# Hybrid S5 and mLSTM trunk: PSUM operands for VectorE, stored high and low parts, and block products on GpSimd

## The chip, the core and the metric

The kernel runs on one core of one Trainium2 chip. A core has TensorE (PE, matrix products), VectorE (DVE, elementwise work with one or two inputs), ScalarE (ACT, one input through a function), GpSimd (POOL, elementwise work) and SyncE (SP, which here only issues DMAs). Operands lie in SBUF or in PSUM. [...]

The metric is the device time of one execution in microseconds (us); lower is better. Every run here is the median of several executions where more than one was made.

## The reference

Two layers, each of one mixer, over 512 tokens of width 1024, all in fp32. Cut to what matters:

```python
h = rms_norm(x, norm_gain) * (1 + scale) + shift          # scale, shift, gate from silu(c) @ w_mod
ssm_in, ssm_gate, m_in, m_o, m_gate = split(h @ w_in)     # 1024 columns each
# S5: 64 groups of 16 channels, each with a complex diagonal state of 64
y = gelu(Re(C @ scan(a, B @ ssm_in)) + d * ssm_in)
y = y * sigmoid(y @ w_glu + b_glu)
ssm_y = rms_norm(y, out_gain) * silu(ssm_gate)
# mLSTM: 4 heads of 256
xc = silu(causal_conv4(m_in) + conv_b)
q, k, v = xc @ wq, xc @ wk / 16, m_in @ wv
i_pre, f_pre = [q|k|v] @ w_gates
num, den = stabilised matrix memory of (q, k, v, i_pre, log_sigmoid(f_pre))
hn = layer_norm(num / max(|den|, exp(-m)) * sigmoid(m_o)) * m_gain
m_y = (hn + skip * xc) * silu(m_gate)
x = x + gate * ([ssm_y | m_y] @ w_out)
```

A last `rms_norm` closes the trunk.

## The kernel before

**Tiling.** Activations are held with channels in the 128 lanes and the 512 tokens along the free axis, eight such tiles for a width of 1024. [...] `split` makes the two parts: ACT writes `hi`, then DVE or POOL subtracts. The low parts of all weights are POOL's. Of the activations, the kinds in the table `LOW` are POOL's, the others DVE's.

**S5.** The recurrence runs over chunks of 8 tokens: 64 chunks, 63 steps in order, each step four DVE operations on 128x64 elements (`scan`). Before it, the powers of `a` are multiplied into B for blocks of 8 groups (`u_prep`, three products and sums on 128x1024: B'), and into C (`u_outp`: C', which waits in DRAM until the output stage). PE forms the chunk inputs from B' (`v5`) and the outputs from C' (`y5`).

**mLSTM.** `min_u` projects, convolves by four taps and applies silu; `v_u` forms v; v and the convolved rows go to DRAM in fp32, and `qk`, `s_u` and `t_u` read them back later; `qk` and `s_u` split them again into high and low parts. `gate_rows` works on 4x512 rows. `pv` ends with a layer norm, whose inverse square root is a Newton iteration on DVE (`rsqrt_steps`).

**GLU.** `y_load`, `glu` and `s_gate` read the S5 output, which is stored by (step in the chunk, chunk), through a view that turns it into token order.

**Order of work.** The work is cut into units, named in the table `ORDER`, one string for each layer: IN and SI (S5 input), MI (mLSTM input), PR (B'), V (chunk inputs), VU and CU (v and convolved rows), CP and CV (C' on POOL and on DVE), GR and GC (gate rows and columns), SC (eight steps of the recurrence), O (output gate), GM and GS (gates of the two branches), QK, SU, PV, TU (the parts of a head), Y (S5 output), YL and GL (GLU), SN and SG (its norm and gate), OM, OS, OA and OB (output projection), MD and MC (adaLN columns), NH (input of the next layer). What a unit does ahead of its first `yield` is issue in an earlier unit's place (`@n`: n units earlier). PE, ACT, POOL and SP run their instructions in just this order; a scheduler sets the order of DVE's. Loads and most stores are issued by SP; a store is issued some units after its data was asked for (the `LAG_` constants), and SP waits there if the data is not ready, with all later loads behind it. Weights are fetched two ahead (`LA`). All PSUM tiles come from one pool of eight banks.

## Time and profile before

| What | Value |
| --- | --- |
| time, median of 3 runs | 1303.7 us (1298.79 to 1307.14) |
| the profiled execution | span 1301.3 us from the first to the last instruction; the page gives no other time of it, and the median lies 2.4 us above this span |
| mean granted TensorE clock | 0.916 |
| busy: PE, DVE, POOL, ACT | 1123.8, 988.9, 612.2, 511.4 us |
| recurrence, layer 0 and layer 1 (first to last step) | 249.6 to 365.0 us, 898.6 to 1000.1 us |
| B' on DVE, layer 0 and layer 1 | 101.9 to 215.8 us, 713.9 to 866.0 us |
| DMA | 213.34 MB, 164 GB/s on average |

The span can be cut by what the kernel does: start (0 to 95 us), input stage of layer 0 (95 to 250), recurrence (250 to 365), heads and S5 output (365 to 520), GLU (520 to 580), output projection (580 to 684), S5 input of layer 1 (684 to 762), its input stage (762 to 898), recurrence (898 to 1000), heads (1000 to 1147), GLU and output projection (1147 to 1301). A view by windows gives each engine's busy time in such stretches. An instruction that has started and is held back by the hardware counts as busy, so a long duration of a small instruction has to be compared with the shortest of its kind.

### The profile page before, as it was taken

Reading aid. Unit: us, or ns where it says so; the run is one execution under the profiler, and the core shown is the slowest. Engines: PE = TensorE matmul, PEld = TensorE weight load, DVE = VectorE, ACT = ScalarE, POOL = GpSimd, SP = SyncE. Lnnn points to the kernel's source line nnn. Section 1 sums busy time; section 2 is a strip of 40 time slices with the busy share of each in tenths; the row PEclk is TensorE's granted clock in tenths of the full one; section 3 lists DMA queues with packets and bytes.
Section 4 is the critical chain, followed back from the end, with each engine's and each line's share of the span. In section 5 each row is a group of like instructions: output and inputs, shape, how many; then the busy total and the mean of one; then the engine's idle time right before and its main releaser. Section 6 shows DMA issues by size and latency. Waiting matters only on the chain.

```text
span 1301.3 us, 17201 instructions
## 1 busy us (share of the span) xinstructions
PE 1123.8 (86%) x6020; PEld 966.2 (74%) x6020; DVE 988.9 (76%) x1892; ACT 511.4 (39%) x821; POOL 612.2 (47%) x333
## 2 busy tenths in 40 slices
...
GB/s 307 155 190 146 135 90 117 164 121 118 257 186 168 155 247 172 267 236 180 73 205 98 93 173 181 118 94 198 198 94 158 208 202 218 194 227 153 123 73 65
DMA packets 274338, 213.34 MB, mean 164 GB/s; under 512 B 63820, under 2 KB 239436, under 8 KB 274252
## 3 DMA queue, kind: packets, MB, share of 16 engines
...
## 4 chain that ended last, share of the span: by engine, by line
PE 36%; DVE 34%; issue 11%; POOL 6%; DMA 5%; SPq 4%; ACT 3%; DVEq 0%; POOLq 0%; ACTq 0%
DVE sc_a L925 4%; DVE st L928 4%; DVE macc L751 2%; DVE cv L799 2%; DMA wr_in<-in_w_in_dram 2%; DVE sc_b L926 2%; DVE sc_a L927 2%; PE ps_ga L411 2%; PE ps_ga L412 2%; PE ps_os L412 2%; PE ps_os L413 2%; PE ps_ga L413 2%; PE ps_os L411 2%; DVE bu L682 2%; PE ps_om L412 2%
## 5 line engine op out<-in xcount | busy, mean ns | idle before, releaser
L127 POOL TENSOR_TENSOR wl_in<-wr_in,wh_in 128x1024 fp32r<-128x1024 f32 x57 | 142.5, 2502 | 279.1 <-ACT wh_in L126 263.9
L126 ACT ACTIVATE wh_in<-wr_in 128x1024 fp32r<-128x1024 f32 x57 | 60.1, 1057 | 118.2 <-DMA wr_in<-in_w_in_dram 83.1
L411 PE MATMUL ps_ga<-hh,wh_in 128*128 128x512 f32 x256 | 104.4, 408 | 0.0
L412 PE MATMUL ps_ga<-hh,wl_in 128*128 128x512 f32 x256 | 102.9, 402 | 0.7 <-POOL wl_in L127 0.7
L413 PE MATMUL ps_ga<-hl,wh_in 128*128 128x512 f32 x256 | 102.4, 400 | 0.0
L411 PE MATMUL ps_o<-wh_o,hh 128*128 128x256 f32 x256 | 73.8, 288 | 14.3 <-ACT wh_o L126 14.3
L413 PE MATMUL ps_o<-wl_o,hh 128*128 128x256 f32 x256 | 74.0, 289 | 6.8 <-POOL wl_o L127 6.8
L412 PE MATMUL ps_o<-wh_o,hl 128*128 128x256 f32 x256 | 73.4, 287 | 0.0
L127 POOL TENSOR_TENSOR wl_o<-wr_o,wh_o 128x1024 fp32r<-128x1024 f32 x16 | 41.1, 2568 | 57.4 <-ACT wh_o L126 47.7
L127 POOL TENSOR_TENSOR vl<-vf,vh 128x1024 fp32r<-128x1024 f32 x8 | 17.6, 2202 | 94.6 <-ACT vh L126 59.9
L411 PEld LDWEIGHTS ps_o<-wh_o,hh 128*128 128x128 f32 x256 | 50.1, 196 | 15.2 <-ACT wh_o L126 14.9
L978 DVE SCALAR_TENSOR_TENSOR gath<-gath,ps_ga 128x512 f32<-128x512 f32 x32 | 21.8, 682 | 50.7 <-ACT gath L977 50.6
L925 DVE TENSOR_TENSOR sc_a<-a8r,st 128x64 f32<-128x64 f32 x126 | 56.8, 451 | 3.9
L412 PE MATMUL ps_gl<-yh,wl_gl 128*128 128x512 f32 x128 | 52.6, 411 | 6.6 <-POOL wl_gl L127 6.6
L412 PEld LDWEIGHTS ps_ga<-hh,wl_in 128*128 128x128 f32 x256 | 49.4, 193 | 11.7 <-POOL wl_in L127 1.1
L413 PEld LDWEIGHTS ps_ga<-hl,wh_in 128*128 128x128 f32 x256 | 49.2, 192 | 11.6
L411 PEld LDWEIGHTS ps_ga<-hh,wh_in 128*128 128x128 f32 x256 | 49.5, 193 | 11.1 <-issue 0.2
L928 DVE TENSOR_TENSOR st<-sc_a,sc_b 128x64 f32<-128x64 f32 x126 | 54.1, 429 | 3.6
L413 PEld LDWEIGHTS ps_o<-wl_o,hh 128*128 128x128 f32 x256 | 49.8, 195 | 7.7 <-POOL wl_o L127 7.7
L412 PE MATMUL ps_mi<-hh,wl_in 128*128 128x512 f32 x128 | 52.2, 408 | 3.7 <-POOL wl_in L127 3.7
L413 PE MATMUL ps_gl<-yl,wh_gl 128*128 128x512 f32 x128 | 52.8, 412 | 2.6 <-DVE yl L127 1.8
L700 PE MATMUL kps<-pair,bt 128*128 128x144 f32 x256 | 42.9, 332 | 13.1 <-DVE pair L691 13.0
...
## 6 DMA issues: line engine op xcount, KB each, us to landing
...
```

Source lines behind the costliest of these rows:

```text
L126: S.activation(out=hi, in_=src, func=AF.Copy)
L127: (eng or V).tensor_tensor(out=lo, in0=src, in1=r32(hi), op=ALU.subtract)
L411: PE.matmul(ps, lhsT=w[0], rhs=a[0], start=first, stop=False)
L412: PE.matmul(ps, lhsT=w[1], rhs=a[0], start=False, stop=False)
L413: PE.matmul(ps, lhsT=w[0], rhs=a[1], start=False, stop=last)
L682: V.tensor_tensor(out=bu, in0=pw_[:, 1, gs, :].unsqueeze(3).to_broadcast(shp), in1=bt_in[:, 1].unsqueeze(2).to_broadcast(shp), op=ALU.mult)
L700: PE.matmul(kps[:, 144 * e:144 * e + 144], lhsT=bt[:, 2 * i + e].rearrange("p k c -> p (k c)"), rhs=pair[:, i, 16 * e:16 * e + 144], start ...
L751: V.scalar_tensor_tensor(out=acc, in0=wt, scalar=silc[:, k:k + 1], in1=acc, op0=ALU.mult, op1=ALU.add)
L799: V.scalar_tensor_tensor(out=cv[:, sh:], in0=xm[:, j, 0:T - sh], scalar=vcol(l, "conv_w", tap * 8 + m), in1=cv[:, sh:], op0=ALU.mult, op1= ...
L925: V.tensor_tensor(out=ta, in0=a8r[:, l], in1=st[:, n - 1], op=ALU.mult)
L926: V.tensor_tensor(out=tb, in0=a8i[:, l], in1=st[:, n - 1, ::-1, :], op=ALU.mult)
L928: V.tensor_tensor(out=st[:, n], in0=ta, in1=tb, op=ALU.add)
```

## The change

1. **One input in PSUM.** Of most DVE operations with two inputs, one input is now a PSUM tile. `scan` copies its two coefficient tiles into a PSUM bank and writes both products there. The convolution reads the projection's PSUM tile, whose bank stays in use until the silu and the split are done. `gate_rows`, the Newton iteration, the attention weights, the GLU products, the head's output products and `next_h` are changed in the same way. [...]
2. **High and low parts in DRAM.** `min_u` and `v_u` split their results at once; v is stored as two tensors and the convolved rows as three (full, high, low). `qk` and `s_u` load the parts and split nothing.
3. **GLU by (step, chunk).** `y_load` and `glu` keep the stored order, and the S5 gate is written in it; the turn into token order is made in `s_gate`.
4. **B' and C' on POOL.** `u_prep` makes B' by five POOL instructions (one product of 128x1024, two of 128x512, two sums of 128x512). All C' blocks are POOL's (CV is gone), and in `ORDER` the C' blocks stand behind the input stage, among the steps of the recurrence.
5. **Moved to ACT.** One tap and the bias of the convolution, the last scaling of the layer norm, and a copy of two S5 inputs to PSUM; ACT's copy of the S5 output is gone.

```diff
 ORDER (layer 0)
-    IN7 F0@5 F2 F1@3 PR0 MI0 F3 MI1 PR1 UB MI2@4 V0 VU0 CP0 PR2 MI3 V1 PR3 MI4 V2@5 VU1 CU0 PR4 MI5@1
+    IN7 F0@5 F2 F1@3 PR0 MI0 F3 MI1 PR1 VU0 UB CU0 MI2@4 V0 PR2 MI3 V1 VU1 PR3 CU1 MI4 V2@5 PR4
...
-LOW = {"p2", "p3", "s0", "v", "wk", "wq", "wv", "xm", "y1"}
+LOW = {"wk", "wq", "wv", "y1"}
...
 def u_prep(l, b):
-        V.tensor_tensor(out=bt, in0=pw_[:, 0, gs, :].unsqueeze(3).to_broadcast(shp),
-                        in1=bt_in[:, 0].unsqueeze(2).to_broadcast(shp), op=ALU.mult)
-        V.tensor_tensor(out=bu, in0=pw_[:, 1, gs, :].unsqueeze(3).to_broadcast(shp),
-                        in1=bt_in[:, 1].unsqueeze(2).to_broadcast(shp), op=ALU.mult)
-        V.tensor_tensor(out=bt, in0=bt, in1=bu, op=ALU.add)
+        GP.tensor_tensor(out=bt, in0=pw_[:, 0, gs, :].unsqueeze(3).to_broadcast(shp),
+                         in1=bc_in[:, 0].unsqueeze(2).to_broadcast(shp), op=ALU.mult)
+        for i in range(2):
...
+            GP.tensor_tensor(out=bu, in0=pw_[:, 1, gh, :].unsqueeze(3).to_broadcast(shh),
+                             in1=bc_in[:, 1, hs_].unsqueeze(2).to_broadcast(shh), op=ALU.mult)
+            GP.tensor_tensor(out=bt[:, hs_], in0=bt[:, hs_], in1=bu, op=ALU.add)
...
 def min_u(m):
-            S.activation(out=xm[:, j], in_=ps, func=AF.Copy)
-            V.tensor_scalar(out=cv, in0=xm[:, j], scalar1=vcol(l, "conv_w", 3 * 8 + m),
-                            scalar2=vcol(l, "conv_b", m), op0=ALU.mult, op1=ALU.add)
+            S.activation(out=xmp[h][0][:, j], in_=ps, func=AF.Copy)
+            S.activation(out=cv, in_=ps, func=AF.Identity, scale=vcol(l, "conv_w", 3 * 8 + m),
+                         bias=vcol(l, "conv_b", m))
+            V.tensor_tensor(out=xmp[h][1][:, j], in0=ps, in1=r32(xmp[h][0][:, j]), op=ALU.subtract)
             for tap in range(3):
-                V.scalar_tensor_tensor(out=cv[:, sh:], in0=xm[:, j, 0:T - sh],
+                V.scalar_tensor_tensor(out=cv[:, sh:], in0=ps[:, 0:T - sh],
...
             yield
-            V.scalar_tensor_tensor(out=xc[h][:, j], in0=th, scalar=1.0, in1=cv, op0=ALU.add, op1=ALU.mult)
+            V.scalar_tensor_tensor(out=ps, in0=ps, scalar=1.0, in1=cv, op0=ALU.add, op1=ALU.mult)
+            yield
+            split(xcp[h][0][:, j], xcp[h][1][:, j], ps)
+            S.activation(out=xc, in_=ps, func=AF.Copy)
+            store(Xd[l][0][h][:, j], xc, LAG_X)
...
 def scan(n0, n1):
+                s5["sc"] = ptile([P, 4, 2, 32], "scp")
...
-                V.tensor_tensor(out=ta, in0=a8r[:, l], in1=st[:, n - 1], op=ALU.mult)
-                V.tensor_tensor(out=tb, in0=a8i[:, l], in1=st[:, n - 1, ::-1, :], op=ALU.mult)
-                V.tensor_tensor(out=ta, in0=ta, in1=st[:, n], op=ALU.add)
-                V.tensor_tensor(out=st[:, n], in0=ta, in1=tb, op=ALU.add)
+                V.tensor_tensor(out=ta, in0=ar, in1=st[:, n - 1], op=ALU.mult)
+                V.tensor_tensor(out=tb, in0=ai, in1=st[:, n - 1, ::-1, :], op=ALU.mult)
+                V.tensor_tensor(out=tv, in0=ta, in1=st[:, n], op=ALU.add)
+                V.tensor_tensor(out=st[:, n], in0=tb, in1=tv, op=ALU.add)
...
 def qk(h):
-            split(xch, xcl, xr, low("xr"))
+            ld(out=r32(xch), in_=Xd[l][1][h])
+            ld(out=r32(xcl), in_=Xd[l][2][h])
...
 def glu(m):
-            V.scalar_tensor_tensor(out=yv, in0=view(th), scalar=1.0, in1=yv, op0=ALU.add, op1=ALU.mult)
+            S.activation(out=ps, in_=ps, func=AF.Tanh, scale=0.25, bias=hb_glu[:, l, m:m + 1])
+            V.scalar_tensor_tensor(out=ps, in0=ps, scalar=1.0, in1=yv, op0=ALU.add, op1=ALU.mult)
...
-            V.scalar_tensor_tensor(out=yv, in0=view(gt), scalar=hgain[:, l, m:m + 1], in1=yv,
+            V.scalar_tensor_tensor(out=yv, in0=gt, scalar=hgain[:, l, m:m + 1], in1=ps,
```

**DVE at the first steps of the recurrence, layer 0.** Before, with the gate rows in between (`row_lf`, `row_m`, `row_i`, `row_b`, `brow`; `sc_a` and `sc_b` are the two products of a step, `st` the states):

```order
L1022 SCALAR_TENSOR_TENSOR row_lf<-row_f,row_la 4x512
L928 TENSOR_TENSOR st<-sc_a,sc_b 128x64
L1023 SCALAR_TENSOR_TENSOR row_m<-row_lf,row_i 4x512
L1024 SCALAR_TENSOR_TENSOR row_b<-row_lf,zeros 4x512
L1028 CAST brow<-zeros 36x512
L1025 TENSOR_TENSOR row_i<-row_i,row_b 4x512
L925 TENSOR_TENSOR sc_a<-a8r,st 128x64
L1026 TENSOR_TENSOR row_b<-row_b,row_m 4x512
L926 TENSOR_TENSOR sc_b<-a8i,st 128x64
```

The same place after, where `scp` is the PSUM tile of the recurrence and `gps` that of the gates:

```order
L1034 SCALAR_TENSOR_TENSOR gps<-gps,row_la 4x512
L1035 SCALAR_TENSOR_TENSOR row_m<-gps,row_i 4x512
L1036 SCALAR_TENSOR_TENSOR gps<-gps,zeros 4x512
L1040 CAST brow<-zeros 36x512
L1037 TENSOR_TENSOR row_i<-row_i,gps 4x512
L1038 TENSOR_TENSOR gps<-gps,row_m 4x512
L933 TENSOR_TENSOR sc_v<-scp,st 128x64
L1041 CAST brow<-gps 4x512
L934 TENSOR_TENSOR st<-scp,sc_v 128x64
```

The gate rows now come within the first step instead of within the eleventh, and each row with two inputs has `gps` or `scp` among them.

**POOL in the input stage of layer 0.** Before, around the low part of the second head's input (`xml`); `wl_in` is the low part of a projection weight, `wvl` that of a v weight, `cp` and `cu` are C':

```order
L127 TENSOR_TENSOR wl_in<-wr_in,wh_in 128x1024
L127 TENSOR_TENSOR xml<-xm,xmh 128x1024
L127 TENSOR_TENSOR wvl<-wv,wvh 128x512
L127 TENSOR_TENSOR wl_in<-wr_in,wh_in 128x1024 x2
L127 TENSOR_TENSOR xml<-xm,xmh 128x1024
```

After, from the second head's v weight on (`bt` and `bu` are B'):

```order
L127 TENSOR_TENSOR wvl<-wv,wvh 128x512
L127 TENSOR_TENSOR wl_in<-wr_in,wh_in 128x1024
L670 TENSOR_TENSOR bt<-pw,bc_in 128x1024
L678 TENSOR_TENSOR bu<-pw,bc_in 128x512
L680 TENSOR_TENSOR bt<-bt,bu 128x512
L678 TENSOR_TENSOR bu<-pw,bc_in 128x512
L680 TENSOR_TENSOR bt<-bt,bu 128x512
L127 TENSOR_TENSOR wl_in<-wr_in,wh_in 128x1024
```

A block of B' now stands between two weights' low parts, and the low part of the head's input has left the queue.

**POOL in the recurrence of layer 0.** Before, between the first four weights of the output gate (`wl_o`) there is one block of C':

```order
L735 TENSOR_TENSOR cp<-cp,cu 128x512
L127 TENSOR_TENSOR wl_o<-wr_o,wh_o 128x1024
L127 TENSOR_TENSOR wl_in<-wr_in,wh_in 128x1024
L127 TENSOR_TENSOR wl_o<-wr_o,wh_o 128x1024
L731 TENSOR_TENSOR cp<-tw,ct_in_2330 128x512
```

After, a second one stands between the third and the fourth:

```order
L734 TENSOR_TENSOR cp<-cp,cu 128x512
L127 TENSOR_TENSOR wl_o<-wr_o,wh_o 128x1024
L127 TENSOR_TENSOR wl_in<-wr_in,wh_in 128x1024
L730 TENSOR_TENSOR cp<-tw,ct_in_2113 128x512
L732 TENSOR_TENSOR cu<-tw,ct_in_2113 128x512
L734 TENSOR_TENSOR cp<-cp,cu 128x512
```

Over the whole recurrence of layer 0 the queue holds eight blocks of C' instead of four; in layer 1 five instead of one.

More of the change, by code (lines that the diff above doesn't have):

```diff
@@ L145, in rsqrt_steps @@
             yield
-    def rsqrt(out, x, shape):
-        for _ in rsqrt_steps(out, x, shape):
-            pass
     ident = const.tile([P, P], F32, name="ident")
@@ L786, in min_u @@
             if j == 0:
-                xms[h] = mt([P, 2, T], name="xm")
-                xc[h] = mt([P, 2, T], name="xc")
+                xmp[h] = mt([P, 2, T], F32R, name="xmh"), mt([P, 2, T], F32R, name="xml")
             w = weight(l, "in", 2 * KT + m)
@@ L859, in v_u @@
         def v_u(h):
-            xmh = mt([P, 2, T], F32R, name="xmh")
-            xml = mt([P, 2, T], F32R, name="xml")
-            split(xmh, xml, xms[h], low("xm"))
+            xmh, xml = xmp[h]
             wv = sw_([P, 2, DH], "wv")
@@ L878, in v_u @@
                             j == 0, j == 1)
-                S.activation(out=v[:, 2 * t2:2 * t2 + 2, :], in_=vps, func=AF.Copy)
-            sto(out=Vd[l][h], in_=v)
+                split(vh[:, 2 * t2:2 * t2 + 2, :], vl[:, 2 * t2:2 * t2 + 2, :], vps)
+            for i, t_ in enumerate((vh, vl)):
+                store(Vd[l][i][h], r32(t_), LAG_V)
             gate_mm(h, 0, xmh, xml)
         def c_u(h):
-            store(Xd[l][h], xc[h], LAG_X)
-            xch = mt([P, 2, T], F32R, name="xch")
-            xcl = mt([P, 2, T], F32R, name="xcl")
-            split(xch, xcl, xc[h], low("xc"))
             yield
-            gate_mm(h, 1, xch, xcl)
+            gate_mm(h, 1, *xcp[h])
+            for i, t_ in enumerate(xcp[h]):
+                store(Xd[l][1 + i][h], r32(t_), LAG_X)
         ub = []
@@ L921, in scan @@
             st = s5["st"]
[L922 to L928 removed]
+            if n0 == 1:
+                s5["sc"] = ptile([P, 4, 2, 32], "scp")
+                V.tensor_copy(out=s5["sc"][:, 0], in_=a8r[:, l])
+                V.tensor_copy(out=s5["sc"][:, 1], in_=a8i[:, l])
+            ar, ai, ta, tb = (s5["sc"][:, i] for i in range(4))
+            for n in range(n0, n1):
+                tv = small.tile([P, 2, 32], F32, tag="sc_v", name="sc_v")
+                V.tensor_tensor(out=ta, in0=ar, in1=st[:, n - 1], op=ALU.mult)
+                V.tensor_tensor(out=tb, in0=ai, in1=st[:, n - 1, ::-1, :], op=ALU.mult)
+                V.tensor_tensor(out=tv, in0=ta, in1=st[:, n], op=ALU.add)
+                V.tensor_tensor(out=st[:, n], in0=tb, in1=tv, op=ALU.add)
             yield
```

184 lines of the change are left out of this document (93 added, 91 removed).

## The prediction

> **What bounds the kernel now.** I read the page's busy times and chain first, then an order-of-time view of DVE and POOL in the recurrence, then the source view of single lines, then the stages by windows.
>
> ```profile
> span 1301.3 us, 17201 instructions
> PE 1123.8 (86%) x6020; PEld 966.2 (74%) x6020; DVE 988.9 (76%) x1892; ACT 511.4 (39%) x821; POOL 612.2 (47%) x333
> PE 36%; DVE 34%; issue 11%; POOL 6%; DMA 5%; SPq 4%; ACT 3%; DVEq 0%; POOLq 0%; ACTq 0%
> ```
>
> PE and DVE share the chain almost equally, so no one engine bounds the whole; the bound changes by stage. The next view shows what a DVE instruction costs in the recurrence (start, duration), quiet first, then beside POOL.
>
> ```profile
> 294.93 0.22 DVE L925 TENSOR_TENSOR sc_a<-a8r,st 128x64 f32<-128x64 f32 x1
> 295.07 0.22 DVE L926 TENSOR_TENSOR sc_b<-a8i,st 128x64 f32<-128x64 f32 x1
> 295.20 0.22 DVE L927 TENSOR_TENSOR sc_a<-sc_a,st 128x64 f32<-128x64 f32 x1
> 295.46 0.23 DVE L928 TENSOR_TENSOR st<-sc_a,sc_b 128x64 f32<-128x64 f32 x1
> 295.71 0.23 DVE L925 TENSOR_TENSOR sc_a<-a8r,st 128x64 f32<-128x64 f32 x1
> ...
> 299.12 2.38 POOL L127 TENSOR_TENSOR wl_in<-wr_in,wh_in 128x1024 fp32r<-128x1024 f32 x1 [8.62 <-ACT wh_in L126]
> 299.16 2.42 DVE L927 TENSOR_TENSOR sc_a<-sc_a,st 128x64 f32<-128x64 f32 x1
> ```
>
> A quiet step takes 0.78 us from start to start. The same instruction, started 0.04 us after a POOL subtraction of 2.38 us, lasts 2.42 us: it stood until POOL was done. Which instructions this strikes is seen from shortest, median and longest duration of a line (ns):
>
> ```profile
> L925 DVE TENSOR_TENSOR sc_a<-a8r,st x126: 206/225/2431, 89.0 to 999.4; 128x64 f32<-128x64 f32 x126
> L964 DVE SCALAR_TENSOR_TENSOR yt<-gq,yt x16: 679/690/1909, 397.7 to 1124.1; 128x512 f32<-128x512 f32 x16
> L978 DVE SCALAR_TENSOR_TENSOR gath<-gath,ps_ga x32: 669/684/691, 232.9 to 1146.3; 128x512 f32<-128x512 f32 x32
> L1274 DVE SCALAR_TENSOR_TENSOR nx<-ps_om,modc,xo x16: 726/740/752, 587.7 to 1248.1; 128x512 f32<-128x512 f32 x16
> ```
>
> The first two read SBUF twice and are held up to 2.4 us; the last two have one input in PSUM and, over 48 instances beside the same POOL, never are. That is what the change makes of most DVE work. What it can bring depends on what stands next in each stage (columns: length; busy PE, weight loads, DVE, ACT, POOL; clock; DMA share; GB/s):
>
> ```profile
> 95.00:250.00 155.00, 132.44 (x730) 117.80 (x731) 119.99 (x166) 59.06 (x102) 66.56 (x32) 0.87 0.56 121
> 250.00:365.00 115.00, 77.57 (x483) 69.24 (x481) 111.21 (x271) 27.07 (x36) 64.42 (x39) 0.83 0.50 165
> 365.00:520.00 155.00, 147.53 (x829) 128.96 (x830) 113.06 (x232) 85.32 (x153) 50.42 (x29) 0.93 0.69 192
> 520.00:580.00 60.00, 51.11 (x199) 39.17 (x198) 56.30 (x64) 24.47 (x32) 34.59 (x15) 0.91 0.80 255
> 762.00:898.00 136.00, 112.70 (x619) 98.04 (x619) 105.64 (x119) 54.48 (x95) 72.59 (x40) 0.91 0.62 133
> 898.00:1000.00 102.00, 82.98 (x529) 74.60 (x527) 97.70 (x277) 29.07 (x39) 40.31 (x21) 0.94 0.49 155
> 1000.00:1147.00 147.00, 139.86 (x804) 122.22 (x805) 103.14 (x221) 84.59 (x155) 55.29 (x30) 0.94 0.76 208
> ```
>
> Both recurrences (second and sixth row) and the GLU of layer 0 (fourth) are DVE's: 111 of 115, 98 of 102, 56 of 60. The heads (third and last) are PE's. In the input stages (first and fifth) neither is full; they hand work to each other.
>
> **The change part by part.** *Recurrence.* Its groups:
>
> ```profile
> L925 DVE TENSOR_TENSOR sc_a<-a8r,st 128x64 f32<-128x64 f32 x126 | 56.8, 451 | 3.9
> L928 DVE TENSOR_TENSOR st<-sc_a,sc_b 128x64 f32<-128x64 f32 x126 | 54.1, 429 | 3.6
> L926 DVE TENSOR_TENSOR sc_b<-a8i,st 128x64 f32<-128x64 f32 x126 | 37.1, 295 | 0.0
> L927 DVE TENSOR_TENSOR sc_a<-sc_a,st 128x64 f32<-128x64 f32 x126 | 34.8, 276 | 1.0 <-ACT st L916 1.0
> ```
>
> Together 182.8 us; quiet, 126 steps of four by 0.22 are 111, so 72 us are waiting for POOL, 36 a layer. DVE falls to 111 − 36 = 75 us in layer 0 and 98 − 36 = 62 in layer 1.
>
> No row of this trace writes PSUM from DVE, so its cost is bounded from both sides. Reading costs nothing: 684 ns with PSUM (L978) against 690 without (L964). At worst each write must have landed before the next instruction starts; the gap after a dependent one is 0.26 us against 0.14 after a free one, so four dependent gaps make a step 1.04 us, 0.26 more, 16 us a layer. A gain beyond zero is excluded, since 0.14 is already the quiet gap. I take zero, by L978; at the upper end DVE has 91 and 78 us, still under what follows.
>
> [...]
>
> What comes late next is POOL. A C' block there is six instructions:
>
> ```profile
> L731 POOL TENSOR_TENSOR cp<-tw,ct_in x26: 1056/1086/2046, 144.4 to 901.9; 128x512 f32<-128x512 f32 x26
> L733 POOL TENSOR_TENSOR cu<-tw,ct_in x26: 1049/1068/2041, 146.4 to 902.9; 128x512 f32<-128x512 f32 x26
> L735 POOL TENSOR_TENSOR cp<-cp,cu x26: 1260/1295/2361, 147.5 to 904.1; 128x512 f32<-128x512 f32 x26
> ```
>
> 2 × (1.09 + 1.07 + 1.30) = 6.9 us. Eight instead of four stand in the recurrence of layer 0, so POOL has 64 + 28 = 92 us there; layer 1 has five instead of one, 40 + 28 = 68. So layer 0 is bounded by POOL at 92, and I take 95, **−20**; layer 1 by PE at 83, taken 87, **−15**.
>
> *Input stages.* DVE loses B':
>
> ```profile
> L682 DVE TENSOR_TENSOR bu<-pw,bt_in 128x1024 f32<-128x1024 f32 x16 | 33.3, 2081 | 0.0
> L684 DVE TENSOR_TENSOR bt<-bt,bu 128x1024 f32<-128x1024 f32 x16 | 28.2, 1765 | 0.0
> L680 DVE TENSOR_TENSOR bt<-pw,bt_in 128x1024 f32<-128x1024 f32 x16 | 23.7, 1482 | 3.9 <-DMA bt_in<-in_s5b_dram 3.9
> ```
>
> 5.3 us a block, 43 us a layer: 120 becomes 77, 106 becomes 63. POOL gains the same products in halves, again 6.9 us a block, 55 a layer; it loses the heads' low parts and two or three C' blocks:
>
> ```profile
> L127 POOL TENSOR_TENSOR xml<-xm,xmh 128x1024 fp32r<-128x1024 f32 x8 | 21.3, 2662 | 36.1 <-ACT xmh L126 36.1
> ```
>
> 10.7 a layer, so layer 0 gets 66.6 + 55 − 10.7 − 14 = 97 and layer 1 72.6 + 55 − 10.7 − 21 = 96, both under PE's 132 and 113. PE becomes the bound, with a few us of handover as in the heads (155 against 147.5): 137 and 118, **−18** and **−18**. The low parts, the silu and the v split now follow each other on DVE, but four or five instructions of 0.7 us a unit fit in DVE's freed 43 us.
>
> *Heads.* `qk` no longer splits; PE's waits for `xcl` go (total, times, longest):
>
> ```profile
> PEld qps L413 <- DVE xcl L127: 24.1, 5, 10.5
> ```
>
> They lie in the heads of both layers, whose gain can't exceed PE's idle, 7.5 and 7.1 us: **−6** and **−3**. The second low part costs loads: 4 heads by 2 × 0.5 MB is 4 MB a layer on 147 us × 208 GB/s = 31 MB. I cost it at nothing, since units ahead cover it and the DMA share would rise from 0.76 to 0.86; uncovered, 4 MB at 208 GB/s is 19 us a layer.
>
> *GLU.* Unstrided, its products should take L978's time:
>
> ```profile
> L1239 DVE SCALAR_TENSOR_TENSOR y<-gt_s,hgain,y 128x512 f32<-128x512 f32 x16 | 26.7, 1672 | 2.5 <-ACT sq L1233 2.5
> L1225 DVE SCALAR_TENSOR_TENSOR y<-gth,y 128x512 f32<-128x512 f32 x16 | 20.8, 1302 | 12.4 <-ACT gth L1223 12.3
> ```
>
> 8 × (0.99 + 0.62) = 13 us less of DVE a layer; layer 0 falls from 60 to PE's 51 and a margin, 54, **−6**; layer 1's GLU is PE's already.
>
> *At nothing:* the start, the output projections and S5 input, whose code barely moves; ACT's new work (39% busy) and the Newton steps and gate rows, short beside PE.
>
> *The clock.* PE ran at 0.87 in the input stage of layer 0 and at 0.93 in the heads, where it pauses less. If the input stages reach 0.93, PE's 132 and 113 shrink by 8 and 2: **−10**.
>
> Sum: 20 + 15 + 18 + 18 + 6 + 3 + 6 + 10 = 96. The profiled span gives 1301 − 96 = 1205, and with the 2.4 us by which the median of the runs lies above it, 1207.
>
> **The rivals.** *PSUM runs out of banks (slower).* `min_u` used to free its bank after one ACT copy; now eight passes over 512 elements hold it (a subtraction, three taps, tanh, the product, the split's two), by L978 and L1274 some 0.7 us each, 5.6 us. Gate rows 1, v 2, chunk inputs 1, B' products and transposes 2, the new S5 copy 1 and two of these make nine, where there are eight. If PE then waits for each bank, 16 units by 5.6 are 90 us, and the heads, whose scores are held for two passes more 32 times, pay 45: 1207 + 135 = 1342. It decides from the point where PE's waits for banks pass the 96 us of the sum; against it speaks that PE has the next unit's whole projection to run meanwhile if one bank is free.
>
> *POOL or the store queue takes the gain.* B' stands ahead of weights' low parts, and SP waits for POOL's and now for v's and the convolved rows' stores, with weight loads behind:
>
> ```profile
> SPq L481 <- POOL cp L735: 92.4, 19, 14.3
> ```
>
> If every second of the 16 B' blocks reaches PE in full, 8 × 6.9 = 55 us are lost: 1262.
>
> *No gain.* If the waits behind POOL were covered by PE all along, only 72 us of cover move and the time stays near 1300. The two recurrences, where PE is idle 37 and 19 us, speak against it.
>
> **How the numbers follow.** The forecast has a chance of 0.73, POOL or stores 0.13, no gain 0.05, banks 0.09. The forecast's own span: all seven stages at their bounds (124 with the clock, 92, 147.5, 51, 111, 83, 140, against 870 now) give 1301 − 122 = 1179, and if the half-clock stretches largely go as well (PE at 0.99 instead of 0.92 where it binds) some 40 less, 1140; with half the gains and 15 us of the extra loads, 1270. The range is 1140 to 1270, which takes in the second case and leaves out the last two and the edges. I count 1% as what a measurement can tell from no change. Faster by over 1%: 0.73 + 0.13, less 0.01 for the second case's edge, 0.85; within 1%: 0.06; slower: 0.09.
>
> **What would show it.** Durations of the recurrence's lines all within 0.2 to 0.35 us, and both recurrences under 100 us; POOL near 90% in layer 0's; PE's share of the chain up and DVE's under 20%; clock in the input stage at 0.9 or more. Wrong would be: products into PSUM much over 0.3 us; PE waiting on DVE's splits of `ps_mi`; SP waiting longer for POOL than the 92 us above; DMA share over 0.9 in the heads.

## The result, and the profile after

The changed kernel takes 1372.7 us (median of 5 runs, 1370.0 to 1380.0) against 1306.0 us (5 runs, 1298.8 to 1307.1) before: a ratio of 1.0532 with a 95% interval of 1.0497 to 1.0566. The forecast was 1207; it is slower by 5%. The profiled execution of the changed kernel has a span of 1378.3 us, 77 more than before.

The page of the changed kernel: span, busy times, and the chain's shares by engine.

```profile
span 1378.3 us, 17386 instructions
PE 1163.5 (84%) x6020; PEld 1000.3 (73%) x6020; DVE 706.5 (51%) x1856; ACT 503.7 (37%) x869; POOL 623.4 (45%) x391
PE 30%; DMA 6%; POOL 6%; DVE 5%; issue 5%; SPq 3%; ACT 3%; ACTq 0%; DVEq 0%; POOLq 0%
```

DVE did what was promised: 282 us less busy, and from 34% of the chain to 5%. Yet PE, with the same 6020 matmuls, is busy 40 us longer and idle 37 us longer. The recurrence's instructions in the view by groups (last figures: busy us, mean ns, idle us before them):

```profile
L931 DVE TENSOR_TENSOR scp<-scp,st 128x64 f32<-128x64 f32 x126 | 29.0, 231 | 3.8
...
L933 DVE TENSOR_TENSOR sc_v<-scp,st 128x64 f32<-128x64 f32 x126 | 28.0, 223 | 4.4 <-ACT st L918 0.5
```

All four durations are quiet, the two left out at 230 and 223 ns: 451, 295, 276 and 429 stood there before. Their starts are further apart, though (start, duration, layer 0):

```profile
320.13 0.23 DVE L931 TENSOR_TENSOR scp<-scp,st 128x64 f32<-128x64 f32 x1
320.40 0.23 DVE L932 TENSOR_TENSOR scp<-scp,st 128x64 f32<-128x64 f32 x1
320.66 0.23 DVE L933 TENSOR_TENSOR sc_v<-scp,st 128x64 f32<-128x64 f32 x1
320.92 0.22 DVE L934 TENSOR_TENSOR st<-scp,sc_v 128x64 f32<-128x64 f32 x1
321.18 0.23 DVE L931 TENSOR_TENSOR scp<-scp,st 128x64 f32<-128x64 f32 x1
```

A step takes 1.05 us from start to start (median of the 90 steps with nothing between), against 0.79 before: two of its four gaps went from 0.14 to 0.27 us. That is 0.26 us a step, 16 us a layer, taken off what the quiet durations gain. The larger loss is elsewhere. The windows of the changed kernel (same columns as before: length; busy PE, weight loads, DVE, ACT, POOL; clock; DMA share; GB/s), input stage, recurrence, heads, GLU of layer 0, then input stage, recurrence, heads of layer 1:

```profile
111.00:300.00 189.00, 149.34 (x787) 130.78 (x786) 65.37 (x146) 71.90 (x131) 81.17 (x55) 0.83 0.54 131
300.00:407.00 107.00, 90.07 (x505) 78.88 (x505) 79.78 (x281) 24.64 (x39) 86.28 (x58) 0.90 0.71 222
407.00:565.00 158.00, 146.73 (x786) 127.44 (x786) 86.82 (x241) 77.82 (x152) 36.71 (x20) 0.90 0.73 211
565.00:616.00 51.00, 46.98 (x199) 37.80 (x200) 37.77 (x36) 19.09 (x28) 32.02 (x16) 0.97 0.88 290
808.00:964.00 156.00, 118.39 (x639) 102.77 (x637) 51.36 (x111) 60.92 (x115) 64.88 (x43) 0.86 0.52 131
964.00:1075.00 111.00, 96.54 (x578) 85.14 (x578) 85.34 (x290) 32.54 (x47) 70.94 (x46) 0.95 0.69 211
1075.00:1222.00 147.00, 135.98 (x721) 121.43 (x722) 80.23 (x214) 73.27 (x143) 34.00 (x18) 0.84 0.72 208
```

The input stages (first and fifth row) have grown to 189 and 156 us although no engine but PE is busy for even half of them, and PE's clock fell there, to 0.83 and 0.86 from 0.87 and 0.91. Something holds all engines at once. The longest waits of SP's queue (total, times, longest):

```profile
SPq L473 <- ACT xc L809: 125.5, 13, 14.3
SPq L473 <- POOL cp L734: 124.2, 29, 9.9
...
SPq L473 <- ACT vh_o L126: 46.8, 7, 12.1
```

And those of PE, the three longest:

```profile
PE vv L403 <- ACT wvh L126: 22.3, 6, 5.8
PE ps_si L403 <- DVE pair L690: 19.3, 1, 19.3
PE vps L914 <- issue: 13.4, 1, 13.4
```

L473 is the line that issues the delayed stores: SP stands there 125 us for convolved rows and 47 us for v's high part (the high part of a value is what ACT writes of it as fp32r, the low part the rest; v's store was ACT's before). PE waits for a weight's high part (`wvh`), for a PSUM bank (`inp`'s, which DVE's `pair` reads last) and before the chunk inputs (`vps`), whose operand `ub` had its last load land at 167.8 us, just before PE went on at 168.2. What SP does before the last of these, in order of time (start, duration):

```profile
114.97 0.42 SPq L447 DMA_DIRECT2D wr_in<-in_w_in_dram  x1
144.52 0.34 SPq L473 DMA_DIRECT2D Xf<-xc  x1
144.96 15.46 SPq L900 DMA_DIRECT2D ub<-Ud  x8
160.52 2.46 SPq L473 DMA_DIRECT2D Vh<-vh_o  x1
```

From 115.4 to 144.5 us SP issues nothing: the store `Xf<-xc` waits for its row, and `ub`'s eight loads stand behind it. PE runs dry at 154.7. The windows there:

```profile
154.70:158.40 3.70, 0.04 (x1) 0.00 (x0) 0.00 (x0) 0.00 (x0) 0.00 (x0) 1.00 1.41 99
158.40:168.20 9.80, 0.04 (x1) 0.07 (x1) 0.00 (x0) 0.00 (x0) 0.00 (x0) 0.50 1.35 152
168.20:182.30 14.10, 10.14 (x38) 9.12 (x39) 4.12 (x8) 4.66 (x9) 10.78 (x8) 0.50 0.72 223
```

For 13 us almost no compute engine works, and PE's clock then stays at half until 182.3. B' comes late as well: POOL stands idle 29.4 us, until 171.4, for the load of `bc_in`, which went out behind `ub` and those stores.

Theories for the experiments: *store queue* (stores of the new rows hold loads in SP's queue), *banks* (PSUM), *order* (the new table), *POOL* (B' ahead of weights' low parts).

### The profile page after: what moved, and what is told of

Read it like the earlier page. It is cut to its first block, busy times and chain, and to the rows that moved or that the text cites. A ratio compares the mean times of both kernels' runs of the same rounds, so it can differ in the third digit from the quotient of the medians.

```text
span 1378.3 us, 17386 instructions
## 1 busy us (share of the span) xinstructions
PE 1163.5 (84%) x6020; PEld 1000.3 (73%) x6020; DVE 706.5 (51%) x1856; ACT 503.7 (37%) x869; POOL 623.4 (45%) x391
## 4 chain that ended last, share of the span: by engine, by line
PE 30%; DMA 6%; POOL 6%; DVE 5%; issue 5%; SPq 3%; ACT 3%; ACTq 0%; DVEq 0%; POOLq 0%
DMA wr_in<-in_w_in_dram 3%; PE ps_om L403 2%; PE ps_om L405 2%; PE ps_om L404 2%; PE ps_os L404 2%; PE ps_os L405 2%; PE ps_os L403 2%; POOL wl_in L127 2%; PE yps L961 1%; PE ps_ga L404 1%; PE ps_ga L403 1%; PE ps_ga L405 1%; PE ps_gl L404 1%; PE ps_gl L403 1%; PE yps L959 1%
## 5 line engine op out<-in xcount | busy, mean ns | idle before, releaser
L127 POOL TENSOR_TENSOR wl_in<-wr_in,wh_in 128x1024 fp32r<-128x1024 f32 x57 | 136.1, 2392 | 265.5 <-ACT wh_in L126 238.0
L126 ACT ACTIVATE wh_in<-wr_in 128x1024 fp32r<-128x1024 f32 x57 | 59.9, 1055 | 141.4 <-DMA wr_in<-in_w_in_dram 111.5
L403 PE MATMUL ps_o<-wh_o,hh 128*128 128x256 f32 x256 | 74.6, 291 | 1.0 <-ACT wh_o L126 1.0
L404 PE MATMUL ps_o<-wh_o,hl 128*128 128x256 f32 x256 | 74.4, 291 | 0.0
L670 POOL TENSOR_TENSOR bt<-pw,bc_in 128x1024 f32<-128x1024 f32 x16 | 31.0, 1935 | 91.1 <-DMA bc_in<-in_s5b_dram 80.2
L794 DVE TENSOR_TENSOR xml<-ps_mi,xmh 128x512 fp32r<-128x512 f32 x16 | 11.0, 690 | 117.3 <-ACT cv L792 117.3
L961 PE MATMUL yps<-sc,cw 128*128 128x64 f32 x256 | 61.5, 330 | 10.7 <-ACT sc L955 10.7
L750 DVE SCALAR_TENSOR_TENSOR macc<-wmod,silc,macc 128x1024 f32<-128x1024 f32 x28 | 55.1, 1969 | 17.4 <-DMA wmod<-in_w_mod_dram 17.3
L959 PE MATMUL yps<-ub,dw 128*128 128x64 f32 x256 | 60.3, 325 | 0.0
L127 POOL TENSOR_TENSOR wl_o<-wr_o,wh_o 128x1024 fp32r<-128x1024 f32 x16 | 38.2, 2394 | 46.0 <-ACT wh_o L126 46.0
L961 PEld LDWEIGHTS yps<-sc,cw 128*128 128x128 f32 x256 | 50.4, 245 | 10.9 <-ACT sc L955 10.9
L403 PE MATMUL ps_gl<-yh,wh_gl 128*128 128x512 f32 x128 | 52.1, 407 | 5.5 <-ACT yh L126 5.5
## 6 DMA issues: line engine op xcount, KB each, us to landing
wmod<-in_w_mod_dram SPq DMA_DIRECT2D x32, 256.0 KB, 6.0
Gd<-gath SPq DMA_DIRECT2D x32, 256.0 KB, 3.0
Cp<-cp SPq DMA_DIRECT2D x32, 256.0 KB, 2.2
```

The costliest lines, as they stand in the source:

```text
L126: S.activation(out=hi, in_=src, func=AF.Copy)
L127: (eng or V).tensor_tensor(out=lo, in0=src, in1=r32(hi), op=ALU.subtract)
L403: PE.matmul(ps, lhsT=w[0], rhs=a[0], start=first, stop=False)
L404: PE.matmul(ps, lhsT=w[1], rhs=a[0], start=False, stop=False)
L670: GP.tensor_tensor(out=bt, in0=pw_[:, 0, gs, :].unsqueeze(3).to_broadcast(shp), in1=bc_in[:, 0].unsqueeze(2).to_broadcast(shp), op=ALU.mult)
L750: V.scalar_tensor_tensor(out=acc, in0=wt, scalar=silc[:, k:k + 1], in1=acc, op0=ALU.mult, op1=ALU.add)
```

## The experiments

Each profiled execution was cut at the same three units in each layer, by PE's rows: the first product of the output gate (O), the first of the GLU (GL) and the last S5 input product of layer 1. Lengths in us, with the ratio to the kernel before; "O units" is the time that the output gate's eight products take in layers 0 and 1, which is where PE works beside the recurrence.

| run | to O | O to GL | GL to layer 1 | to O | O to GL | to the end | O units | ratio (95%) |
| --- | --- | --- | --- | --- | --- | --- | --- | --- |
| before | 246.1 | 273.4 | 242.4 | 134.9 | 250.0 | 154.5 | 100.7, 91.5 | 1 |
| after | 285.7 | 267.6 | 241.7 | 161.3 | 264.0 | 157.9 | 88.4, 89.1 | 1.0532 (1.0497 to 1.0566) |
| e1 | 285.1 | 260.8 | 242.0 | 165.7 | 262.8 | 160.1 | 86.2, 88.3 | 1.0554 (1.0523 to 1.0585) |
| e2 | 253.4 | 260.4 | 244.2 | 135.9 | 259.3 | 162.7 | 87.1, 91.2 | 1.0094 (1.0064 to 1.0123) |
| e3 | 289.7 | 249.0 | 242.5 | 175.7 | 237.3 | 162.3 | 73.0, 74.1 | 1.0426 (1.0397 to 1.0454) |
| e4 | 286.3 | 258.7 | 233.9 | 165.2 | 263.3 | 158.0 | 86.1, 88.9 | 1.0508 (1.0481 to 1.0535) |
| e5 | 244.8 | 269.2 | 242.6 | 128.1 | 262.8 | 157.9 | 90.6, 88.4 | 0.9987 (0.9966 to 1.0007) |
| e6 | 246.8 | 263.6 | 242.3 | 130.0 | 262.4 | 158.1 | 90.5, 88.8 | 0.9967 (0.9946 to 0.9988) |
| e7 | 267.8 | 252.3 | 241.7 | 142.9 | 248.0 | 159.9 | 79.2, 78.0 | 1.0051 (1.0028 to 1.0074) |
| b1 | 245.1 | 257.8 | 241.2 | 134.6 | 237.7 | 155.9 | 75.5, 74.6 | 0.9735 (0.9710 to 0.9761) |
| b2 | 257.3 | 257.0 | 248.8 | 148.5 | 238.4 | 154.2 | 80.4, 74.9 | 1.0000 (0.9978 to 1.0022) |
| c1 | 243.8 | 256.6 | 235.7 | 134.3 | 239.6 | 160.1 | 72.4, 74.0 | 0.9730 (0.9709 to 0.9751) |
| c2 | 253.8 | 260.9 | 235.5 | 138.9 | 259.2 | 161.8 | 88.4, 86.9 | 1.0068 (1.0053 to 1.0083) |
| c3 | 253.0 | 254.9 | 233.8 | 148.8 | 245.2 | 161.8 | 73.3, 78.7 | 0.9987 (0.9967 to 1.0007) |
| d1 | 256.0 | 256.0 | 234.7 | 144.3 | 241.4 | 158.5 | 73.0, 74.3 | 0.9890 (0.9846 to 0.9934) |
| d2 | 246.1 | 257.5 | 233.6 | 141.6 | 238.9 | 160.4 | 73.2, 74.1 | 0.9803 (0.9773 to 0.9832) |
| d5 | 245.1 | 264.8 | 239.0 | 139.1 | 244.1 | 159.2 | 75.7, 75.2 | 0.9868 (0.9823 to 0.9913) |
| d3 | 257.8 | 252.8 | 232.6 | 144.7 | 241.8 | 162.4 | 74.4, 74.4 | 0.9951 (0.9919 to 0.9984) |
| f4 | 243.0 | 264.7 | 234.5 | 134.6 | 253.9 | 158.9 | 69.6, 74.9 | 0.9898 (0.9866 to 0.9929) |
| f3 | 243.7 | 260.8 | 231.9 | 134.5 | 244.1 | 158.7 | 76.4, 74.4 | 0.9765 (0.9740 to 0.9789) |

A difference of two ratios is given in us below, times 1304 us (the time before was 1303.4 to 1306.3 us in these sets).

### e1: the bank of `inp`

```diff
-        inp = ptile([P, 2, GB, CG], "inp")
-        S.activation(out=inp, in_=bc_in[:, 2:4], func=AF.Copy)
...
-        c0u = inp[:, 1]
+        c0u = small.tile([P, GB, CG], F32, tag="c0u", bufs=1, name="c0u")
```

> The C' input of each S5 block is read from SBUF again; the PSUM tile inp and its ACT copy are gone (2 times 8 tiles less in PSUM), all else as in the changed kernel. Theory banks: inp takes the eighth bank in the start, and PE waits 19.3 us for DVE's pair to give it back; the wait goes, 7 to 19 us of it are gained (the fold of the gate weights may wait for its loads there instead, as before the change), with some more from banks in the later blocks and from the clock: 1335 to 1365, and PE waits for the pair less than 5 us in the start. Theory store queue, theory order, theory POOL: the wait in the start only moves, and the time stays within 5 us of 1372.

No change (1376.1 us). PE's waits of this run:

```profile
PE gm L835 <- issue: 13.1, 1, 13.1
...
PE vps L912 <- issue: 12.8, 1, 12.8
```

The bank's 19.3 us are gone, and PE waits 13.1 us at the fold of the gate weights (`gm`) in their place, then for `ub` as before. The bank was a wait in front of another wait, so the bank of `inp` is not the main cause.

### e2: three stores off SP's queue

```diff
-            store(Xd[l][0][h][:, j], xc, LAG_X)
+            sto(out=Xd[l][0][h][:, j], in_=xc)
...
+            sto(out=Vd[l][0][h], in_=r32(vh))
+            store(Vd[l][1][h], r32(vl), LAG_V)
...
+            sto(out=Xd[l][1][h], in_=r32(xcp[h][0]))
+            store(Xd[l][2][h], r32(xcp[h][1]), LAG_X)
```

> The stores of xc, of the high part of the convolved input and of the high part of v are issued by ACT, which writes them, and no longer stand in SP's queue; all else as in the changed kernel. Theory store queue: SP's waits for ACT's xc (125 us) and vh (47 us) go, weight loads and the loads of the S5 blocks go out earlier, PE's waits for ub (13.4 us), wvh and wvl (30 us) shrink, and the clock with them: 1320 to 1345. Theory banks, theory order, theory POOL: SP has slack, the time stays at 1365 to 1378.

1316.5 us: 57 us faster, by (1.0532 − 1.0094) × 1304, with the same bytes, the same arithmetic and the same PSUM tiles; so the banks are not what these 57 us cost. Of the 62.5 us between the two profiled spans 57.7 lie in the two input stages (285.7 to 253.4 and 161.3 to 135.9). The input stage of layer 0 in its window:

```profile
111.00:268.00 157.00, 138.54 (x791) 121.89 (x791) 66.17 (x147) 72.33 (x131) 81.36 (x56) 0.92 0.64 157
```

The same 790 matmuls in 157 us instead of 189, the clock at 0.92 instead of 0.83. `ub`'s loads now begin at 116.2 us, not 145.0. The longest wait for a new row that is left in SP's queue is for the low part of v:

```profile
SPq L473 <- DVE vl_o L127: 122.0, 7, 19.6
```

### e3 and e7: the order of before

```diff
-    IN7 F0@5 F2 F1@3 PR0 MI0 F3 MI1 PR1 VU0 UB CU0 MI2@4 V0 PR2 MI3 V1 VU1 PR3 CU1 MI4 V2@5 PR4
+    IN7 F0@5 F2 F1@3 PR0 MI0 F3 MI1 PR1 UB MI2@4 V0 VU0 CP0 PR2 MI3 V1 PR3 MI4 V2@5 VU1 CU0 PR4 MI5@1
...
```

Both tables are those of the kernel before, with its CV (C' on DVE) read as CP (C' on POOL).

> The order of the units is that of the kernel before (the C' blocks that DVE had in it are on POOL), all else as in the changed kernel. Theory order: the earlier fold and convolution units and the C' blocks in the recurrence cost the time; 1320 or less. Theory banks: the wait of the start stays (inp is still in PSUM), 1360 to 1390. Theory store queue: stores of C' stand in the queue in the input stage again, 1370 to 1400.

1358.9 us, 14 us faster. It is a trade: the stretches from O to GL fall by 19 and 27 us, the O units from 88 to 73, where fewer C' blocks stand among the recurrence's steps (four instead of eight in layer 0, one instead of five in layer 1); the input stages, which get them back, grow by 4 and 14 us.

> As the run with the stores of xc, xch and vh on ACT (1316.5 us), with the order of the kernel before. Under the full set of stores in SP's queue the order was worth 13 us. Theory order by itself: 13 us here too, 1300 to 1306. Theory that the order counts only through the queue (it sets what stands behind a store): 1312 to 1322.

(e7 is e2 with that table.) 1313.3 us, 6 us faster than e2 by the ratios, with intervals that overlap: the same trade, now nearly even (input stages +14 and +7, O to GL −8 and −11). The order is not the main cause. The C' blocks were not moved by themselves in any run, so that they make the trade is argued.

### e4: B' on DVE again

```diff
-        GP.tensor_tensor(out=bt, in0=pw_[:, 0, gs, :].unsqueeze(3).to_broadcast(shp),
+        V.tensor_tensor(out=bt, in0=pw_[:, 0, gs, :].unsqueeze(3).to_broadcast(shp),
...
```

The same is done to the four other instructions of B'.

> B' of each S5 block is computed on DVE again, in the same three products; all else as in the changed kernel. Theory POOL (B' ahead of weights' low parts in POOL's queue): PE's waits for POOL's wl, wvl and bt (some 45 us in all) shrink by half or more and the time falls to 1340 to 1355. Theory banks or store queue: DVE gets 43 us a layer back in the input stages, the time stays or grows, 1365 to 1400.

1370.2 us, within the uncertainty of the changed kernel: while SP's queue holds the input stage, it does not matter who makes B'.

### e5 and e6: no store of the new rows on SP, then `inp` in SBUF too

```diff
-            store(Vd[l][1][h], r32(vl), LAG_V)
+            store(Vd[l][1][h], r32(vl), 4, sto)
```

The last argument is the issuing queue; `xcl`'s store is changed in the same way.

> As the run with the stores of xc, xch and vh on ACT (1316.5 us), and the stores of the low parts vl and xcl are issued by ACT too, four units after their split, so that SP's queue holds no store of the new rows at all. Theory store queue: SP's remaining waits for DVE's vl (122 us in 7 waits) go, PE's waits for wvh and wvl (13 us) shrink: 1295 to 1308. If what is left is not the queue: 1312 to 1320; if ACT waits for DVE's low parts in its own queue instead: over 1322.

1304.5 us, 14 us below e2; its input stages are 16 us shorter. With the queue freed, the changed kernel is back at the time before, not below it.

> As the run with no store of the new rows in SP's queue, and inp in SBUF again. Theory banks, in its weaker form (the bank wait of the start was masked while the queue held the loads behind it): 8 to 15 us faster than that run. If the bank of inp costs nothing even then, since the fold's loads end at the same time: within 4 us of it.

1302.3 us; the intervals of e5 and e6 overlap. The bank of `inp` costs nothing that can be measured, also without the queue.

### b1: the recurrence alone

The kernel before with only `scan` changed, to the function of the changed kernel.

> The kernel before with only the recurrence's constants and products in PSUM (one bank more held from its first step), all else as before. The prediction's part on the recurrence: its four instructions fall to 0.2 to 0.23 us, the recurrence of layer 0 ends 10 us or more earlier and the time falls by 8 to 20: 1284 to 1296. Theory that DVE's contention there was covered, or that POOL and SP bound the stage: 1298 to 1306. Theory banks: 1310 or more.

1271.6 us, 35 us faster than before. But the recurrence itself hardly shortens: its steps run from 248.1 to 360.6 us, against 249.6 to 365.0. Its instructions are busy 31 us less in layer 0 (56 against 87), but a quiet step takes 1.05 us here too, and DVE does more other work between the steps (46 us against 28). What shortens is PE's work beside it, the O units, from 100.7 and 91.5 us to 75.5 and 74.6. Of PE's waits before,

```profile
PE qps L413 <- DVE xcl L127: 22.0, 5, 10.0
PE ps_o L411 <- ACT wh_o L126: 14.3, 2, 12.7
...
PE cps L1039 <- DVE sc_a L925: 9.7, 1, 9.7
```

the second is gone in b1, the third is 0.2 us and the first 12.0: what PE waited for was work that came late behind the recurrence, not its end. How this reaches PE is seen at the 12.7 us for `wh_o`. SP's longest single wait beside layer 0's recurrence, before and then in b1:

```profile
SPq L481 <- DVE sc_b L926: 23.0, 1, 23.0
SPq L481 <- DVE scp L930: 13.4, 1, 13.4
```

Both times SP stands before the store of a gate's row (`gath`). Before, ACT had that row ready at 302.6 us, but DVE multiplied it only at 319.2, between the recurrence's steps; its store went out at 319.9 and the load of `wr_o`, next in SP's queue, at 320.4; that landed at 324.3, ACT made `wh_o`, and PE went on at 325.4. In b1 the same store goes out at 295.2 and the load at 295.6. So this part of the gain of `scan`, too, comes through SP's queue.

### c1: all PSUM inputs behind the input stage

The changed kernel with `min_u`, `v_u`, `c_u`, `u_prep`, `u_outp`, the loads of `qk` and `s_u` and the order of the kernel before.

> The changed kernel with the input stage (convolution, v, the stored rows and their splits), B', C' and the order of the kernel before: of the change it keeps the PSUM inputs in the recurrence, the S5 output, the GLU by step and chunk, scores, gates, norms and the next layer's h. Theory that the edits behind the input stage gain what the prediction says (GLU 6 us, a few more where DVE is freed): 1252 to 1268. Theory banks (scores, head transposes and GLU products hold theirs longer) or ACT (head norms and splits moved there): 1275 to 1290.

1269.6 us. b1 has 0.9735 and this 0.9730: all the edits behind the recurrence, the GLU by (step, chunk) among them, are together worth nothing that can be measured. The GLU's products in layer 0 are 6 us shorter than in b1 (554.4 − 500.4 = 54.0 us against 59.9), those of layer 1 6 us longer (60.6 against 54.7). c1 and b1 are the fastest kernels of this study and beat both given ones.

### b2 and c2: B' on POOL, without and with the rest

b2 is b1 with the three instructions of B' on POOL:

```diff
-        V.tensor_tensor(out=bt, in0=pw_[:, 0, gs, :].unsqueeze(3).to_broadcast(shp),
+        GP.tensor_tensor(out=bt, in0=pw_[:, 0, gs, :].unsqueeze(3).to_broadcast(shp),
...
```

> The kernel before with the recurrence's constants and products in PSUM (1271.6 us) and the three products of B' on GpSimd (whole blocks, in the order of the kernel before; C' as before). The prediction's part on the input stages (DVE loses 43 us a layer and PE becomes the bound): each input stage 10 to 18 us shorter, 1236 to 1252. Theory POOL (B' stands ahead of weights' low parts and the PE waits there): input stages as long or longer, 1268 to 1290.

1305.5 us: moving B' to POOL costs 35 us where the convolution still reads SBUF twice, and loses all that the recurrence gained. DVE's view by groups in the input stage of layer 0, b1 and then b2:

```profile
L799 DVE SCALAR_TENSOR_TENSOR cv<-xm,vec,cv 128x509 f32<-128x509 f32 (+2 forms) x24 | 22.8, 949 | 0.5
L691 DVE TENSOR_TENSOR pair<-c,c0u 128x128 f32<-128x128 f32 x8 | 4.4, 552 | 0.0
```

```profile
L799 DVE SCALAR_TENSOR_TENSOR cv<-xm,vec,cv 128x509 f32<-128x509 f32 (+2 forms) x24 | 37.7, 1569 | 0.6
L691 DVE TENSOR_TENSOR pair<-c,c0u 128x128 f32<-128x128 f32 x8 | 11.8, 1480 | 0.2
```

And the window of that stage in b2:

```profile
95.00:257.00 162.00, 133.84 (x695) 118.51 (x696) 117.13 (x146) 55.93 (x99) 112.07 (x54) 0.83 0.52 113
```

DVE gave away 43 us of B' and stayed busy 117 us of the stage, against 121 in b1: its convolution taps went from 949 to 1569 ns. In b2 15 of the 24 taps take over 1.4 us, against 6 in b1; six of the 15 started within a B' product of POOL, six within its C' blocks and three within its low parts. In the kernel before, the 32 taps beside no POOL instruction took at most 0.753 us, and 15 of the 16 beside one took 1.42 to 2.77; in the changed kernel, where a tap reads PSUM, 29 of the 48 ran beside POOL's products and subtractions, and none took over 0.752. Not all 35 us were traced to this: in that stage PE's waits for POOL rise as well, from 2.5 to 8.5 us, and its clock falls from 0.87 to 0.83.

c2 is e6 with the five instructions of B' on DVE, the edit of e4.

> As the run with no store of the new rows in SP's queue and inp in SBUF (1302.3 us), with B' on DVE again. Theory POOL (now that the queue no longer hides it, B' on POOL delays weights' low parts): 1282 to 1292. Theory that B' is equally dear on both engines: 1298 to 1306; that DVE binds again: 1308 or more.

1313.9 us, 13 us slower than e6: where the taps read PSUM (c2, e6), POOL is the better place for B'. It seems that the two edits need each other, though the pairs b1, b2 and c2, e6 differ in more than the taps (order, stores, low parts); together with a free queue they come out even with before.

### c3: the new input stage, with B', C' and the order of before

It is e2 with `u_prep`, `u_outp` and both tables of the kernel before.

> The changed kernel with B', C' and the order of the kernel before, and the stores of xc, xch and vh on ACT: against the run with the order of before and these stores (1313.3 us) only B' and C' change their engine, against the run without the new input stage only the input stage and the stored parts come in. If B' and C' on POOL make up what the changed kernel still loses to the scan alone: 1275 to 1290. If it is the input stage and the stored parts: 1300 to 1318, with SP waiting over 80 us for vl.

1302.3 us, 33 us above c1, and in the profiles 24 of 27 us lie in the two input stages (253.0 against 243.8, 148.8 against 134.3). PE now waits for banks of v that DVE's low parts hold:

```profile
PE ps_mi L403 <- DVE vl_o L127: 18.1, 4, 5.9
```

### d3: v copied out of its bank

```diff
-                split(vh[...], vl[...], vps)
+                v = st_([P, 2, DH], name="v")
+                S.activation(out=v, in_=vps, func=AF.Copy)
+                split(vh[...], vl[...], v, GP)
```

> As the run with the changed input stage, B', C' and the order of before, and the stores of xc, xch and vh on ACT (1302.3 us), with v copied from its PSUM bank to SBUF by ACT and vl computed by POOL from there, so that the bank is free after one copy. Theory banks: PE's wait for the bank of v that DVE's vl holds (18.1 us in 4) goes: 1282 to 1292. If the bank isn't what the new input stage costs: 1298 to 1306.

1297.6 us, 5 us less by the ratios, with an interval that overlaps c3's: inconclusive. What the new input stage costs beside the queue stays open. Part of it is the stores left on SP in c3 (vl alone holds SP 89 us there; taking vl and xcl off gave e5 14 us); banks and the extra 21 MB were not told apart.

### d1: one old store put into SP's queue

```diff
 c1, v_u:
-            sto(out=Vd[l][h], in_=v)
+            store(Vd[l][h], v, 1)
```

> The kernel with the old input stage and the PSUM inputs behind it (1269.6 us), v's four stores a layer moved from ACT's queue to SP's, a unit after v; not a byte or an instruction else. Theory store queue: SP waits for v and holds weight loads: 1278 to 1295. If a store in that queue costs nothing and the 56 us came from another effect of moving them (DMA queues sharing the engines otherwise): 1266 to 1273.

1290.8 us, 21 us slower, from eight stores that move to another queue: 12.2 us in the first input stage and 10.0 in the second, nothing elsewhere.

```profile
SPq L473 <- ACT v L870: 57.5, 5, 20.6
```

With e2 this shows the cost from both sides. Both runs also move bytes from one engine's DMA queue to another's; that the wait itself is what costs rests also on the 29 us in which SP issued nothing (after). The same stores left on SP but issued some units later were not tried.

### d2, d5 and f3: taking other waits out of the queue

d2 is c1 with POOL's C' blocks stored by POOL; d5 is d2 with the gates' stores on ACT; f3 is c1 with the convolved input's store on ACT:

```diff
+            GP.dma_start(out=Cp[l][:, gs, :], in_=cw.rearrange("p g k c -> p g (k c)"))
...
-            store(Gd[l][which, m * P:(m + 1) * P, :], th, LAG_G)
+            store(Gd[l][which, m * P:(m + 1) * P, :], th, 4, sto)
...
-            store(Xd[l][h], xc[h], LAG_X)
+            store(Xd[l][h], xc[h], 2, sto)
```

> The kernel with the old input stage and the PSUM inputs behind it (1269.6 us), with the stores of the C' blocks that POOL computes issued by POOL itself; SP's waits for POOL's C' (96.6 us in 20) go. Theory store queue: weight loads of the recurrences and the input stages go out earlier: 1250 to 1264. If SP has slack there (weights are loaded two units ahead): 1266 to 1273; if POOL loses more by issuing them: over 1275.

> As the run with C' stores issued by POOL, and the gates' stores issued by ACT four units later; SP's waits for DVE's gates (62.7 us in 13) go too. Theory store queue: 5 to 15 us below that run. If SP has slack in the heads, where PE is busy: within 4 us of it; if ACT now waits for DVE's gates ahead of its own work: slower than it.

> The kernel with the old input stage and the PSUM inputs behind it (1269.6 us), the four stores of the convolved input a layer moved from SP's queue to ACT's, two units after they are ready to go. Theory store queue, every wait dear: SP's 28.6 us of waits for xc go, 1255 to 1264. If only waits with a load of the next few us behind them are dear, and xc's are not such: 1266 to 1273. If ACT now waits for DVE's xc: over 1275.

1281.0, 1290.0 and 1275.1 us: none gains; d2 and d5 lose 9.5 and 18 us, f3 is not told apart from c1. So taking a wait out of SP's queue is not always a gain. In d2, SP's wait for POOL's C' (97 us) goes, but its waits for DVE's gates rise from 63 to 79 us: SP arrives at the next late entry sooner. And POOL pays 0.58 us for each store that it issues, 15 us in all:

```profile
L729 POOL DMA_DIRECT2D Cp<-cp x26: 580/580/722, 146.8 to 887.2; - x26
```

In d5 SP stands 37 us before a load (L343) until a gate's row has been stored, which its buffer waits for. f3 tests less than was expected of it. Of SP's waits for `xc`, c1 and then f3:

```profile
SPq L666 <- DVE xc L796: 27.4, 4, 13.1
SPq L666 <- DVE xc L796: 36.7, 4, 17.6
```

L666 is not the store but the load of `bt_in`, whose buffer comes from the same pool as the convolution's rows; the store of `xc` itself held SP for only 6.8 us in c1. Loads that stood without a free buffer held the queue as late stores did, here for 27.4 and 36.7 us.

### f4: DVE's other work moved behind the recurrence

c1 with the eight MD units of each recurrence, and the MC behind them, spread over the heads in `ORDER`:

```diff
-    SC1 MD020 MD021 O2 GC SC2 CP4 GM2 SC3 O3@2 MD023 O4 GM3 SC4 MD022 CP5 GM4 MD024 GM6 SC5 MD025 O5@5
+    SC1 O2 GC SC2 CP4 GM2 SC3 O3@2 O4 GM3 SC4 CP5 GM4 GM6 SC5 O5@5
...
```

> The kernel with the old input stage and the PSUM inputs behind it (1269.6 us), with the eight 2 us modulation sums that DVE does between the steps of each recurrence spread over the heads behind it. If DVE's other work between the steps sets the recurrence's length (109 and 101 us, of which its own instructions 57): it ends 10 to 17 us earlier in each layer, PE's wait for the S5 state (18.8 us) goes, 1250 to 1262. If POOL's queue sets it: it ends as before, 1266 to 1273; if the heads pay for the sums in full: 1275 or more.

1291.4 us, 22 us slower than c1. The recurrence does end earlier, after 101.1 and 92.3 us (from 245.7 to 346.8 and 879.4 to 971.7) against 108.9 and 101.4 in c1: DVE's work between the steps is part of its length. But the heads pay more for the sums than the recurrence gains (O to GL +8 and +14).

## Why the prediction was wrong, step by step

**The step that failed** is that the sum puts the stores of the new rows at nothing. They are named only in the rival "POOL or the store queue", and there without a price, since that counts POOL's blocks alone. They cost 57 us (e2), or 71 with the low parts (e5), and take the time past that before. A store one unit after its row does not wait long only if the row is done in one unit; here PE, ACT and DVE each work on it in turn, and SP stood up to 14 us for it.

**Input stages, −18 and −18: wrong.** That DVE would be relieved was right, more than I said (120 to 65 us in layer 0). That PE would then bind was not, and this step fails apart from the stores: with the row stores off SP the time to O is 244.8 us against 246.1, and 128.1 against 134.9 in layer 1 (e5), −1 and −7. In the form of b2 the same step costs 35 us.

**Recurrence, −20 and −15: the right sum, by luck.** b1 gains 35 us, from quiet instructions as forecast. But the gain is PE's, in the O units; the steps themselves still take 113 and 101 us, against 115 and 102. The C' blocks that I let POOL carry at 95 and 87 us do cost there: O units of 86 to 91 us with them (after, e1, e2, e4 to e6), 73 to 79 in e3 and e7, with the order of before. Mis-sized, since in b1 and c1, without the move, PE needs only 72 to 76.

**PSUM writes at zero: mis-sized.** By durations it holds (median 232 ns for a product into PSUM, 218 and 225 into SBUF before). By starts a step costs 0.26 us more, 16 us a layer: the upper end that I priced and set aside on the evidence of L978, which shows durations alone. Whether the PSUM write makes the gap, or that both products now lie in one tile, so that the second waits for the first, no run tells apart.

**GLU −6, heads −6 and −3: no net gain.** GLU of layer 0 gained 6 (c1), layer 1's lost 6; PE's waits for `xcl` in `qk` are gone from the changed kernel, but its O to GL in layer 1 is 14 us longer, with C' in it.

**The clock, −10: the other way.** 0.83 in the input stage of layer 0, where PE was idle for 39.7 of 189 us (22.6 of 155 before); 0.92 once the stores were moved, with 18.5 of 157 idle (e2).

**Extra loads at nothing: not refuted.** e2 carries all of the 21 MB more and stands 1% above before; whether they are part of c3's 33 us is open.

**Banks, 1342 with a chance of 0.09: wrong mechanism at nearly the right time.** PE did wait 19.3 us for a bank, `inp`'s and not `ps_mi`'s, and removing it changed nothing (e1, e6).

**What was to show it.** The recurrence's lines were at 0.22 to 0.23 us, but the recurrences took 107 and 111 us, not under 100. DVE's chain share fell to 5%, but PE's fell too, from 36% to 30%; POOL was at 81% of layer 0's recurrence, not near 90. SP's wait for POOL rose from 92 to 124 us, the sign given for wrong; the 125 us for `xc` beside it were not on that list.

The sum from before to after, by ratios in one line of runs (× 1304 us): recurrence −35 (b1), the PSUM inputs behind it −1 (c1), the new input stage with three stores on ACT +34 (c3), B' and C' on POOL and `inp` +8 (e7), the order +6 (e2), the three stores on SP +57 (after): +69. The −1 and the +6 are within the intervals.
